# A planned one-core kernel: one fp32 product becomes a transpose with its mean taken on the vector engine, and the planner that writes the order is changed

## The chip, the core and the metric

The kernel runs on one core of a Trainium2 chip. Five engines work side by side and take their own instructions strictly in the order in which they stand: TensorE (PE in the profile; PEld is its weight load), VectorE (DVE), ScalarE (ACT), GpSimd (POOL) and SyncE (SP, which here only issues DMAs). The metric is the device time of one execution in microseconds (us). Before the change it was 2356.49 us, the median of three runs (2355.05 to 2359.45).

## The reference

One decoder layer on 4096 tokens of width 1024, in float32. The input is normalised and projected once; two groups of heads read the projection, their gated outputs are concatenated, projected back, added to the input and normalised.

```python
u = rmsnorm(x, norm_w) @ w_in
# group 1: 4 heads of gated linear attention, chunked
o = gla(q, k, v, decay); gla_out = rms(o) * gla_norm_w * silu(gg)
# group 2: 8 heads of RWKV-7, head size 64
S_t = S_{t-1} (diag(w_t) - kk_t^T (a_t * kk_t)) + v_t^T k_t ;  y_t = S_t r_t
mu = mean(y); var = mean((y - mu)**2)          # over the 64 values of a head
y = (y - mu) * rsqrt(var + eps) * ln_w + ln_b
bonus = sum(r * k * r_k) * v
rwkv_out = (y + bonus) * silu(rg)
out = rmsnorm(x + concat(gla_out, rwkv_out) @ w_out, final_norm_w)
```

Since y is linear in v, the mean over a head's 64 values of y may be taken out of v ahead of the recurrence: with v minus its mean over the 64 values, y comes out with mean zero.

## The kernel before

The 4096 tokens go in 8 blocks of 512 (`TB`). Activations lie transposed, features on partitions. Every projection is three fp16 products (high by high, high by low, low by high), so x and each weight tile are split into a high and a low half; the weights are split once at the start, partly kept in SBUF and otherwise written to DRAM tiles `wdr`, from which they are loaded again for each block into `wr`, `wg` and `wo`. x's two halves of 8 feature tiles lie in four tiles `x16_i_k` of two feature tiles each.

The RWKV heads go in pairs: a unit `u` (0 to 31) is a block and a pair of heads. For a unit, `rwkv_ab` projects k, r, v and the gate, forms scaled keys and queries (`bk`, `DD`), multiplies them (`bank<-DD,bk`), masks the result into `Nb`, and has the triangular 32x32 blocks inverted: `Nb` goes out to DRAM as `nd` and comes back regrouped as `f`, 31 steps of two operations each (`tm`, `Tc`) run on POOL (on DVE for the last unit), and the result goes through `td` back into `Nb`. `rwkv_i` joins the 32x32 blocks to 64x64. `rwkv_c` is the recurrence over the unit's 8 chunks of 64 tokens: per chunk three small fp32 products (`ch<-sv,DD`, `ch<-us,Nb`, `ch<-uv,bk`) with copies on ACT and DVE between them; the states stand in `sv`, and two passes (`y<-DD,sv`, `y<-Nb,uv`) then make y. Unit u+1's chunks need the state that unit u left.

v enters there: `rwkv_ab` takes v (features on partitions), and for each of its four 128-token pieces makes one fp32 product with the constant `c64`, the 64x64 matrix I - 1/64 on the diagonal of a 128x128 tile. That transposes the piece and takes the mean out in one step; four ACT copies then carry the bank into `sv`.

The order of the instructions is not written by hand. The kernel's streams are run once with a model of the engines (`account`, `place`, `Array`); every instruction becomes a `Step` with its duration, its lag and the steps on which it depends. `forward` is a list schedule: it walks through time and lets each engine take the ready step of best rank; `backward` makes ranks from an end time. Before, one forward pass and 13 rounds of backward and forward are made, and the schedule with the earliest modelled end is written out. `parts` says which pieces of a tile the model holds apart: halves of partitions, and for the tiles in `HEADS` also two halves of columns. `keep` (2.0) is how much rank TensorE gives up to stay in the same tile size; `look` (0.15) is how far ahead DVE and ACT look for a better step. All SP entries are DMAs; the model gives each an issue time on SP and a lag until the data can be used. Nearly every instruction is issued by one helper, so the profile shows one line (L408 before, L433 after) and tiles tell them apart.

The last block's output projection (`out_last`) is done in parts: the six feature tiles that are ready first (`bank<-x,wo`, with `halves` scaling them), then the two tiles of the last heads (`bank<-x,x`).

Of the kernel before, what the change touches and what calls it, by code (L numbers as in the profile page):

```python
# [10 lines left out]
F32 = mybir.dt.float32  # L11
# [70 lines left out]
def hymba_kernel(ctx, tc, xT, wt, wg, wo, wua, gup, pk, ck, out):  # L82
# [16 lines left out]
    TABLES = ("pkt", "scl", "invs", "hinv", "mu_s", "omu_s", "carry", "wosc", "woinv", "gnh", "lnh")  # L99
    HEADS = set()  # L100
    now = [0.0]
# [15 lines left out]

# [47 lines left out]
    def account(eng, out, ins, d, lag, cols=0, tiles=None):  # L165
        rdy = lambda k: (lambda r: r[0] - (r[1] == eng) * {"V": 0.075, "S": 0.1, "G": 0.18}.get(eng, 0.0))(ready.get(k, (0.0, "")))
        t = max([0.0] + [rdy(k) for a in ins for k in parts(a)]
                + [used.get(k, 0.0) for k in parts(out)]
                + [rdy(k) for k in parts(out) if eng != "T"])
        if eng == "T":  # L170
            t0, d = array.put(max(t, now[0]), d, cols, tiles)
            t, now[0] = t0, array.free
        else:
            if eng == "D":
                t0 = place("H", t, 0.63)
                t = t0 + 1.28
# [12 lines left out]
    last, turn = [None, 0], [0]  # L189

# [20 lines left out]
    def put(t0, eng, d, lag, cols, tiles, tab, outs, ins, f):  # L211
# [7 lines left out]
        s = Step(len(steps), t0, eng, d, lag, cols, tiles, tab, f)  # L219
        got = lambda m: m.lag + SPARE * (m.eng == "D") - (m.eng == eng) * {"V": 0.075, "S": 0.1, "G": 0.18}.get(eng, 0.0)  # L220
        for k, timed in ki.items():
# [23 lines left out]
    def forward(rank):  # L245

# [3 lines left out]
        left, ready, start = [len(s.on) for s in steps], [0.0] * len(steps), [0.0] * len(steps)  # L250
        end = [0.0] * len(steps)
        for s in steps:
# [7 lines left out]
        for _ in steps:  # L260
# [5 lines left out]
            if e == "T":  # L266
                x = next((x for x in can[e] if run and x[1] == run.n), None)
                x = x or min(heapq.nsmallest(12, can[e]), key=lambda x: x[0] - 2.0 * (steps[x[1]].form == pes.form))
                run = steps[x[1]].next
                can[e].remove(x)  # L270
                heapq.heapify(can[e])
            else:
                x = can[e][0]
                soon = []
                while e in "VS" and wait[e] and wait[e][0][0] <= t + 0.15:
# [12 lines left out]
            if e == "T":  # L288
                start[s.n], d = pes.put(t, d, s.cols, s.tiles)
                end[s.n] = start[s.n] + d  # L290
            elif e == "D":
                free["H"], free["D"] = t + 0.63, max(t + 1.28, free["D"]) + d
                end[s.n] = free["D"]
            else:
# [11 lines left out]
    def backward(end):  # L306
# [7 lines left out]
        for _ in steps:  # L314
# [7 lines left out]
            if e == "T":  # L322
                hold, form = s.d * s.form[0] * s.form[1] / 16 + 0.09 * (s.form != form), s.form
            elif e == "D":
                hold, long = max(0.63, s.d), s.d + 1.28
            free[e], late[s.n] = t + hold, t + long
# [7 lines left out]
    def cost(eng, op, ins, n, o, acc=False):  # L334
# [32 lines left out]
    class Engine:  # L367
# [5 lines left out]
        def __getattr__(self, op):  # L373
            f = getattr(self.eng, op)

            def call(*a, **kw):
# [3 lines left out]
                if aps:  # L380
# [84 lines left out]

    xp = [[sb(big, [P, 2, 2, TB], F16, f"x16_{i}_{k}") for k in range(KT // 2)] for i in range(2)]
    x16 = [[x[k // 2][:, k % 2] for k in range(KT)] for x in xp]
    mfree = {k: [sb(big, [P, TB], F32, f"mg{k}{i}") for i in range(n)] for k, n in NM.items()}
# [14 lines left out]
    bones = sb(one, [P, 32], F32, "bones")  # L483
    c64 = sb(one, [P, P], F32, "c64")
    G.memset(c64, 0.0)
    smask = sb(one, [P, TB], U8, "smask")
# [346 lines left out]
    def rwkv_ab(u, p, b, xs, LR):  # L833
# [511 lines left out]
    def setup():  # L1345
# [28 lines left out]
        for i, t in enumerate(("crs", "rgs")):  # L1374
# [7 lines left out]
            V.tensor_scalar_mul(usc[:, 4 + i:5 + i], usc[:, 2 * i + 1:2 * i + 2], 0.5 / 16384 if i == 0 else 0.5)  # L1382
        for q in (slice(0, 64), slice(64, 128)):
            D.dma_start(c64[q, q], ck[q, CK_C64:CK_C64 + 64])

# [89 lines left out]
    with tc.manual_schedule(engines={getattr(mybir.EngineType, e) for e in ("PE", "DVE", "Activation", "Pool", "SP")}):  # L1475
# [5 lines left out]
        run()  # L1481
        start, end = forward([s.t0 for s in steps])
        start, end = best = forward(backward(end))
# [69 lines left out]
```

## Time and profile before

| | |
|---|---|
| median of 3 runs | 2356.49 us |
| the profiled execution | 2357.35 us |
| its span, first to last instruction | 2355.5 us |
| mean granted TensorE clock | 0.979 of full |
| PE busy | 2245.6 us, 95% |
| DVE busy | 1664.7 us, 71% |
| ACT busy | 1251.0 us, 53% |
| POOL busy | 842.1 us, 36% |
| DMA | 325.46 MB, mean 138 GB/s |
| the chain that ended last | PE 68%, DVE 19%, DMA 5% |

Busy time of PE is time in which at least one product is under way; single products overlap, so the mean duration of one is longer than the time that it adds. The groups list gives for each kind of instruction its count, the busy time that it adds and the mean of one. The windows view gives the same by stretch of the span, with the granted clock.

### The profile page before, as it was taken

How to read it: one execution, taken by the hardware profiler on the slowest of the kernel's cores; microseconds unless marked ns; L12 is line 12 of the kernel's file. 1: busy time of each engine (PE TensorE's matmuls, PEld its weight loads, DVE VectorE, ACT ScalarE, POOL GpSimd, SP SyncE). 2: the span in 40 equal slices, each digit the busy share in tenths (PEclk: the TensorE clock that was granted, in tenths of full speed). 3: DMA queues.
4: the chain of work that ended last, by engine and by line, in shares of the span. 5: the costliest groups of instructions: out<-in, count | busy, mean ns of one | idle time of the engine just before them, and what ended most of it. 6: DMA issues, size and time to landing. Idle time of an engine off the chain costs nothing.

```text
span 2355.5 us, 52166 instructions
## 1 busy us (share of the span) xinstructions
PE 2245.6 (95%) x19432; PEld 1390.7 (59%) x19432; DVE 1664.7 (71%) x3737; ACT 1251.0 (53%) x3229; POOL 842.1 (36%) x2213
## 2 busy tenths in 40 slices
PE   6888999999999999999999999999999989999986
PEld 3556565556665666656575566655666556755643
DVE  7868768478764786757766787638877677676756
ACT  7566765454654655544654546535564455544442
POOL 3450333524334352235425342342514353321400
PEclk9989999999999999999999999999999999999989
DMA  6666545355334543345424553345533454334432
GB/s 195 204 217 213 158 154 157 113 169 152 103 106 125 179 151 93 109 137 174 141 85 121 175 160 97 102 133 173 153 94 106 123 184 137 97 118 127 130 86 76
DMA packets 275523, 325.46 MB, mean 138 GB/s; under 512 B 131732, under 2 KB 132932, under 8 KB 275268
## 3 DMA queue, kind: packets, MB, share of 16 engines
q1 hardware_dynamic: 275268, 322.13, 45.0%
q8 instruction: 152, 2.49, 0.4%
q14 instruction: 103, 0.84, 0.1%
HBM read 276.97 MB, written 45.05 MB: 137 GB/s over the span
## 4 chain that ended last, share of the span: by engine, by line
PE 68%; DVE 19%; DMA 5%; issue 3%; ACT 2%; POOL 2%; SPq 1%; DVEq 0%; ACTq 0%; POOLq 0%
PE bank L408 60%; PE ch L408 6%; PE y L408 2%; DVE DD L408 2%; DVE nta L408 2%; DVE bk L408 1%; POOL tm L408 1%; POOL Tc L408 1%; DVE mgg L408 1%; DVE mgr L408 1%; SPq L408 1%; DMA wdr<-wo 1%; DVE Nb L408 1%; DVE crs L408 1%; DVE sv L408 1%
## 5 line engine op out<-in xcount | busy, mean ns | idle before, releaser
L408 PE MATMUL bank<-x,wr 128*128 128x512 f16 x3264 | 803.1, 380 | 12.5 <-DVE rk L408 4.7
L408 POOL TENSOR_TENSOR tm<-Tc,f 128x60 f32<-128x60 f32 (+24 forms) x961 | 332.4, 346 | 762.3 <-DMA f<-nd 586.0
L408 PEld LDWEIGHTS <-wr 128*128 128x128 f16 x3264 | 317.0, 100 | 308.0 <-issue 21.4
L408 PE MATMUL bank<-x,wg 128*128 128x512 f16 x1536 | 389.6, 383 | 2.4 <-DMA wg<-wdr 2.0
L408 POOL TENSOR_TENSOR Tc<-Tc,tm 128x60 f32<-128x60 f32 (+24 forms) x961 | 341.6, 355 | 73.4
L408 PE MATMUL bank<-x,wo 128*128 128x512 f16 x1488 | 361.9, 384 | 0.6 <-ACT bk L408 0.6
L408 DVE SCALAR_TENSOR_TENSOR sv<-ch,PC,psd 64x64 f32<-64x64 f32 x448 | 126.2, 282 | 195.9 <-PE ch L408 191.0
L408 POOL TENSOR_TENSOR xacc<-xacc,xr 128x512 f32<-128x512 f32 x98 | 131.3, 1340 | 314.8 <-ACT xr L408 215.3
L408 PEld LDWEIGHTS <-wg 128*128 128x128 f16 x1536 | 148.5, 101 | 147.4 <-issue 11.6
L408 PEld LDWEIGHTS <-wo 128*128 128x128 f16 x1488 | 146.0, 101 | 139.9 <-issue 8.0
L408 PEld LDWEIGHTS <-x 128*128 128x128 f16 x3120 | 189.9, 100 | 27.6 <-issue 12.2
L408 PE MATMUL bank<-wg,x 128*128 128x128 f16 x3072 | 199.6, 222 | 4.5 <-DMA wg<-wdr 4.5
L408 ACT ACTIVATE psd<-sv,PC 128x128 f32<-128x128 f32 x256 | 102.2, 399 | 190.1 <-DVE sv L408 152.9
L408 ACT COPY uv<-ch 64x64 f32<-64x64 f32 x512 | 105.5, 206 | 120.5 <-PE ch L408 114.8
L408 ACT COPY us<-ch 64x64 f32<-64x64 f32 x512 | 105.3, 206 | 103.7 <-PE ch L408 93.3
L408 PEld LDWEIGHTS ch<-sv,DD 128*128 128x128 f32 x512 | 91.9, 192 | 49.3 <-DVE sv L408 20.3
L408 PEld LDWEIGHTS ch<-us,Nb 128*128 128x128 f32 x512 | 92.3, 192 | 40.0 <-ACT us L408 10.5
L408 PEld LDWEIGHTS ch<-uv,bk 128*128 128x128 f32 x512 | 92.4, 192 | 39.6 <-ACT uv L408 12.5
L408 PE MATMUL ch<-sv,DD 128*128 128x128 f32 x512 | 105.9, 289 | 8.7 <-DVE sv L408 6.6
L408 ACT ACTIVATE sa<-bank,mu_s 128x512 f32<-128x512 f32 x104 | 71.5, 688 | 73.5 <-PE bank L408 68.5
L408 PE MATMUL ch<-uv,bk 128*128 128x128 f32 x512 | 103.4, 284 | 4.1 <-ACT uv L408 4.0
L408 POOL MEMSET Tc<- 32x8 f32 (+1 forms) x160 | 23.7, 148 | 223.3 <-DMA td<-Tc 182.2
(332 smaller groups left out, 3670.9 us busy)
## 6 DMA issues: line engine op xcount, KB each, us to landing
wr<-wdr SPq DMA_DIRECT2D x256, 256.0 KB
wg<-wdr SPq DMA_DIRECT2D x184, 256.0 KB
xr<-in_xT_dram SPq DMA_DIRECT2D x176, 256.0 KB
wo<-wdr SPq DMA_DIRECT2D x128, 256.0 KB
f<-nd SPq DMA_DIRECT2D x128, 128.0 KB
x<-in_wt_dram SPq DMA_DIRECT2D x29, 512.0 KB
wdr<-wo SPq DMA_DIRECT2D x25, 512.0 KB
out_dram<-mgg SPq DMA_DIRECT2D x33, 256.0 KB
```

What stands on the lines that cost most here:

```text
L408: put(t0, self.name, d, lag, cols, tiles, tab, outs, ins, lambda: f(*a, **kw))
```

## The change

Five things change.

1. In `rwkv_ab` the four products with `c64` become four transposes against the identity. The mean is then taken out on DVE: a reduction of the bank over each 64 values into `vm` (128x8), and one scalar_tensor_tensor that adds -1/64 of it to the bank in place. `c64`, its memset on POOL and its two DMAs go.
2. `put` makes every DMA from an input wait in the model until x's first eight loads have been placed (`lead`).
3. `parts` knows the four parts of an `x16` tile apart (`XS`): two feature tiles by high and low half.
4. The model's figures change: an issue on SP costs 0.5 us (0.63), a DMA 1.15 us more (1.28), the lags depend on what is loaded (reloaded weights 1.1 us instead of 1.6), at most 8 DMAs are under way, POOL's operations cost 0.09 us more, and results that pass between DVE, ACT and TensorE count as ready a little earlier (`early`).
5. After the first pass, five pairs of `keep` and `look` are tried with ten rounds each, and the best of all is taken.

```diff
+        if ap.tensor.name in XS:
+            o = ap.offset % (4 * TB) // TB
+            e = range(o, o + max(1, math.prod(ap.shape[1:]) // TB)) if ap.dtype == F16 else range(4)
+            return [(ap.tensor.name, h, 2 + i) for h in hs for i in e]
...
+    def early(a, b):
+
+        if a not in "VSGT" or b not in "VSGT" or not a:
+            return 0.0
+        if a == b:
+            return {"V": -0.075, "S": -0.1, "G": -0.18, "T": 0.0}[a]
+        return -0.045 if a == "T" else -0.09 if b == "T" else -0.07
...
+        if eng == "D" and ins[0].tensor.name.startswith("in_"):
+            if ins[0].tensor.name.startswith("in_xT") and len(lead) < KT:
+                lead.append(s)
+            else:
+                for m in lead:
+                    s.follow(m, None)
...
-                free["H"], free["D"] = t + 0.63, max(t + 1.28, free["D"]) + d
+                if len(flight) > 7:
+                    start[s.n] = t = max(t, flight[-8])
+                free["H"], free["D"] = t + 0.5, max(t + 1.15, free["D"]) + d
...
-            return 0.14 + 0.07 * few + n * (2.13 if len(big) > 1 else 0.95) / 960 + 0.34 * (n == 8)
+            return 0.23 + 0.07 * few + n * (2.13 if len(big) > 1 else 0.95) / 960 + 0.34 * (n == 8)
...
-                        d, lag = max(0.01, b / 3.6e5), 1.6 if ins[0].space == DRAM else 0.6
+                        d = max(0.01, b / 3.6e5)
+                        if ins[0].space == DRAM:
+                            lag = {"wdr": 1.1, "in": 1.9 if b > 4e5 else 1.1, "td": 1.2}.get(ins[0].tensor.name.split("_")[0].rstrip("0123456789"), 1.7)
+                        else:
+                            lag = 2.1 if b > 2e5 else 1.2 if o.shape[-1] == 32 else 0.6
...
         for c in range(4):
-            T.matmul(pv[:, c], lhsT=v[:, P * c:P * c + P], rhs=c64, start=True, stop=True)
-
+            T.transpose(pv[:, c].rearrange("p h t -> p (h t)"), v[:, P * c:P * c + P], ident)
+        vm = sb(rt, [P, 8, 1], F32, "vm", 1)
+        pu = pv.rearrange("p c h t -> p (c h) t")
+        V.tensor_reduce(vm, pu, op=ALU.add, axis=AX.X)
+        V.scalar_tensor_tensor(pu, vm.broadcast_to((P, 8, 64)), -1.0 / 64, pu, ALU.mult, ALU.add)
...
-        for _ in range(12):
-            start, end = forward(backward(end))
-            best = min(best, (start, end), key=lambda x: max(x[1]))
+        first_order = forward([s.t0 for s in steps])
+        best = first_order
+        for keep, look in ((0.5, 0.15), (0.5, 0.3), (0.7, 0.3), (1.0, 0.15), (2.0, 0.3)):
+            start, end = first_order
+            for _ in range(10):
+                start, end = forward(backward(end), keep, look)
+                best = min(best, (start, end), key=lambda x: max(x[1]))
```

The whole order is new, on every engine. Three places of it follow.

SP at the program's start, before. `mgg` and `mgr` hold x's eight feature tiles of block 0, `x_1_..` two raw weight tiles.

```order
L408 DMA mgg_0_88<-in_xT_dram 128x512
L408 DMA x_1_0_0_80<-in_wt_dram 128x1024
L408 DMA mgr_0_89<-in_xT_dram 128x512
L408 DMA x_1_1_0_81<-in_wt_dram 128x1024
L408 DMA mgr_0_90<-in_xT_dram 128x512
L408 DMA mgr_0_91<-in_xT_dram 128x512
L408 DMA f_0_216<-in_wg_dram 128x8x16
```

The same place after the change.

```order
L433 DMA mgg_0_88<-in_xT_dram 128x512
L433 DMA mgr_0_89<-in_xT_dram 128x512
L433 DMA mgr_0_90<-in_xT_dram 128x512
L433 DMA mgr_0_91<-in_xT_dram 128x512
L433 DMA x_1_0_0_80<-in_wt_dram 128x1024
L433 DMA x_1_1_0_81<-in_wt_dram 128x1024
L433 DMA f_0_215<-in_wg_dram 128x8x16
```

The two weight tiles of 512 KB have moved behind x's last three tiles of 256 KB.

DVE some 20 us into the program, before: `nva`, `nyg` and `nta` are x's inverse norm by Newton steps, `amW`, `pw` and `scl` a weight tile's scale, `wr<-x_1` the low half of a split weight.

```order
L408 TENSOR_SCALAR nva_207<-bank_0_183 128x128
L408 TENSOR_SCALAR nyg_208<-nva_207 128x128
L408 TENSOR_TENSOR nta_209<-nyg_208 128x128
L408 TENSOR_REDUCE amW_210<-bank_0_183 128x1
L408 TENSOR_SCALAR pw_206<-amW_210 128x1
L408 TENSOR_SCALAR pw_206<-pw_206 128x1
L408 SCALAR_TENSOR_TENSOR wr_215<-x_1_1_0_81,scl_179,wr_214 128x1024
L408 TENSOR_SCALAR scl_179<-pw_206 128x1
L408 SCALAR_TENSOR_TENSOR nta_209<-nta_209,nva_207 128x128
```

The same after the change.

```order
L433 TENSOR_SCALAR nva_206<-bank_0_182 128x128
L433 TENSOR_SCALAR nyg_207<-nva_206 128x128
L433 TENSOR_TENSOR nta_208<-nyg_207 128x128
L433 SCALAR_TENSOR_TENSOR nta_208<-nta_208,nva_206 128x128
L433 SCALAR_TENSOR_TENSOR nyg_207<-nta_208,nyg_207 128x128
L433 TENSOR_TENSOR nta_208<-nyg_207 128x128
```

The Newton steps have moved ahead of the weights' scales and splits; both `wr` splits now stand between the Newton steps and the first use of x's norm.

PE near the program's end, before: the first chunks of unit 30 (`ch`), with v's last product (`c_0,v`), the gates' projections (`wg`) and the output projection (`wo`).

```order
L408 MATMUL ch_266<-us_267,Nb_0_135 128x64
L408 LDWEIGHTS wg_233
L408 MATMUL bank_0_186<-x_1_3_0_83,wg_233 128x512
L408 MATMUL bank_0_183<-c_0_99,v_201 128x128 x3
L408 MATMUL ch_266<-uv_134,bk_242 128x128
L408 MATMUL bank_0_183<-c_0_99,v_201 128x128
L408 MATMUL ch_266<-sv_255,DD_0_132 128x128
L408 MATMUL ch_266<-us_267,Nb_0_135 128x64
L408 MATMUL ch_266<-uv_134,bk_242 128x128
L408 MATMUL ch_266<-sv_255,DD_0_132 128x128
```

The same chunks after the change, from the end of the first one.

```order
L433 MATMUL ch_266<-uv_133,bk_241 128x128
L433 LDWEIGHTS wr_212
L433 MATMUL bank_0_182<-x_1_3_0_83,wr_212 128x512
L433 MATMUL ch_266<-sv_254,DD_0_131 128x128
L433 MATMUL bank_0_183<-ident_102,amo_281 128x128
L433 MATMUL ch_266<-us_267,Nb_0_134 128x64
L433 MATMUL ch_266<-uv_133,bk_241 128x128
L433 LDWEIGHTS wo_138
L433 MATMUL bank_0_187<-x_0_0_0_76,wo_138 128x512
L433 LDWEIGHTS wo_139
L433 MATMUL bank_0_186<-x_0_0_0_76,wo_139 128x512
L433 MATMUL ch_266<-sv_254,DD_0_131 128x128
```

Before, chunks two to four of unit 30 stand without other products between them and the first `wo` product comes in the fifth; after, the first `wo` products stand in the second chunk and go on between the chunks from there.

More of the change, by code (lines that the diff above doesn't have):

```diff
@@ L99, in hymba_kernel @@
     TABLES = ("pkt", "scl", "invs", "hinv", "mu_s", "omu_s", "carry", "wosc", "woinv", "gnh", "lnh")
-    HEADS = set()
+    HEADS, XS = set(), set()
     now = [0.0]
@@ L174, in account @@
             if eng == "D":
-                t0 = place("H", t, 0.63)
-                t = t0 + 1.28
+                t0 = place("H", t, 0.5)
+                t = t0 + 1.15
             t = place(eng, t, d)
@@ L185, in account @@
         return t0
+    def early(a, b):
[4 more added lines that the diff above has]
+        return -0.045 if a == "T" else -0.09 if b == "T" else -0.07
     table = [0]
     steps, wkey, rkey, wlast, readers = [], {}, {}, {}, {}
-    last, turn = [None, 0], [0]
+    last, turn, lead = [None, 0], [0], []
     def whole(ap):
@@ L250, in forward @@
         left, ready, start = [len(s.on) for s in steps], [0.0] * len(steps), [0.0] * len(steps)
-        end = [0.0] * len(steps)
+        end, flight = [0.0] * len(steps), []
         for s in steps:
@@ L267, in forward @@
                 x = next((x for x in can[e] if run and x[1] == run.n), None)
-                x = x or min(heapq.nsmallest(12, can[e]), key=lambda x: x[0] - 2.0 * (steps[x[1]].form == pes.form))
+                x = x or min(heapq.nsmallest(12, can[e]), key=lambda x: x[0] - keep * (steps[x[1]].form == pes.form))
                 run = steps[x[1]].next
@@ L274, in forward @@
                 soon = []
-                while e in "VS" and wait[e] and wait[e][0][0] <= t + 0.15:
+                while e in "VS" and wait[e] and wait[e][0][0] <= t + look:
                     r, n = heapq.heappop(wait[e])
@@ L291, in forward @@
             elif e == "D":
-                free["H"], free["D"] = t + 0.63, max(t + 1.28, free["D"]) + d
+                if len(flight) > 7:
+                    start[s.n] = t = max(t, flight[-8])
+                free["H"], free["D"] = t + 0.5, max(t + 1.15, free["D"]) + d
                 end[s.n] = free["D"]
+                flight.append(end[s.n] + s.lag)
             else:
@@ L324, in backward @@
             elif e == "D":
-                hold, long = max(0.63, s.d), s.d + 1.28
+                hold, long = max(0.5, s.d), s.d + 1.15
             free[e], late[s.n] = t + hold, t + long
@@ L466, in hymba_kernel @@
     xp = [[sb(big, [P, 2, 2, TB], F16, f"x16_{i}_{k}") for k in range(KT // 2)] for i in range(2)]
+    XS.update(t.tensor.name for x in xp for t in x)
     x16 = [[x[k // 2][:, k % 2] for k in range(KT)] for x in xp]
@@ L483, in hymba_kernel @@
     bones = sb(one, [P, 32], F32, "bones")
-    c64 = sb(one, [P, P], F32, "c64")
-    G.memset(c64, 0.0)
     smask = sb(one, [P, TB], U8, "smask")
@@ L1481, in hymba_kernel @@
         run()
-        start, end = forward([s.t0 for s in steps])
-        start, end = best = forward(backward(end))
-        for _ in range(12):
-            start, end = forward(backward(end))
-            best = min(best, (start, end), key=lambda x: max(x[1]))
+        first_order = forward([s.t0 for s in steps])
[5 more added lines that the diff above has]
+                best = min(best, (start, end), key=lambda x: max(x[1]))
         start, end = best
```

8 lines of the change are left out of this document (3 added, 5 removed).

## The prediction

> **What bounds the kernel now.** I read the page first, then the busy time by stretch, then the groups, the waits and the timeline at both ends.
>
> ```profile
> span 2355.5 us, 52166 instructions
> PE 2245.6 (95%) x19432; PEld 1390.7 (59%) x19432; DVE 1664.7 (71%) x3737; ACT 1251.0 (53%) x3229; POOL 842.1 (36%) x2213
> ...
> core 0: us, PE busy (x) PEld busy (x) DVE busy (x) ACT busy (x) POOL busy (x), PEclk, DMA share, GB/s
> 0.00:24.00 24.00, 10.86 (x83) 5.98 (x84) 12.38 (x45) 11.69 (x18) 10.28 (x32) 1.00 0.93 294
> 24.00:80.00 56.00, 48.47 (x235) 23.05 (x234) 51.63 (x133) 40.19 (x73) 16.28 (x13) 0.91 0.46 141
> 80.00:300.00 220.00, 196.36 (x1776) 129.15 (x1775) 177.03 (x470) 145.91 (x321) 78.69 (x201) 0.93 0.63 197
> 300.00:2200.00 1900.00, 1862.91 (x16243) 1154.79 (x16241) 1325.70 (x2840) 999.77 (x2670) 715.48 (x1912) 0.99 0.44 134
> 2200.00:2250.00 50.00, 47.65 (x504) 31.65 (x503) 37.30 (x100) 15.93 (x35) 21.37 (x55) 0.99 0.28 79
> 2250.00:2300.00 50.00, 41.83 (x301) 25.53 (x300) 25.62 (x76) 22.29 (x73) 0.00 (x0) 0.81 0.37 100
> 2300.00:2355.00 55.00, 37.51 (x303) 20.59 (x301) 35.03 (x78) 15.26 (x41) 0.00 (x0) 0.90 0.21 72
> ```
>
> The columns are the stretch, its length, and each engine's busy time with its instructions. From 300 to 2200 us TensorE is busy 98% of the time (1862.9 of 1900): there the kernel is TensorE's work, and work taken from it shortens the span unless a new wait replaces it. TensorE's idle time lies mostly at the ends: 13 us before 24 us, 31 from 24 to 300, 25 after 2250, where the granted clock also falls to 0.81. From 24 to 80 us DVE is busy 92% of the time. So there are three limits: DVE at the start, TensorE in the middle, and a chain of dependent steps at the end.
>
> **v's products become transposes.** The old product is the group `c,v`; `ident,bk` is a transpose of the same size that the kernel already makes.
>
> ```profile
> L408 PE MATMUL bank<-c,v 128*128 128x128 f32 x256 | 37.0, 278 | 0.0
> L408 PE MATMUL bank<-ident,bk 128*128 128x128 f32 x256 | 37.8, 277 | 2.2 <-DVE DD L408 2.2
> ...
> 2252.20 0.83 PE L408 MATMUL bank<-c,v 128*128 128x128 f32 x6
> ...
> 2229.21 0.82 PE L408 MATMUL bank<-ident,bk 128*128 128x128 f32 x6
> ```
>
> A unit makes 4 products, so 32 units make 128, and they have 256 rows: an fp32 product runs as two. A unit makes 8 transposes of `bk`, 256 in all, with 256 rows: one each. By busy time a product costs 37.0/128 = 0.289 us and a transpose 37.8/256 = 0.148. The change saves 128 x 0.141 = 18.1 us by this count. The timeline gives the other bound: six rows in a run take 0.83 and 0.82 us, of which the last one's own 0.28 is tail, so a row adds 0.11 us in either group, a product two rows, a transpose one: 128 x 0.11 = 14.1 us. I take 16, the middle, since the four stand in short runs. It all lies in TensorE's full stretch or in the first 300 us. The constant's memset and two DMAs go as well, from POOL and SP, where TensorE waits for neither. The Trainium skill, "TensorE: Matmul & The Clock Gate", section Terms, says that transpose mode is four times faster for FP32; by it a transpose would cost 0.072 us and the saving be 27.8. The trace says half, not a quarter, and the trace has the kernel's own transposes.
>
> **The mean on DVE.** New per unit: a reduction of 128x512 from PSUM, and one scalar_tensor_tensor that reads and writes PSUM.
>
> ```profile
> L408 DVE TENSOR_REDUCE amW<-crs 128x1 f32<-128x512 f32 x1 | 0.7, 676 | 0.0
> L408 DVE SCALAR_TENSOR_TENSOR rgs<-rgs,bank 128x512 f32<-128x512 f32 x32 | 21.9, 683 | 28.1 <-ACT rgs L408 27.8
> L408 DVE SCALAR_TENSOR_TENSOR r<-r,pkt,kf 128x512 f32<-128x512 f32 x32 | 26.2, 818 | 0.1
> ...
> PE bank L408 <- DVE bk L408: 14.7, 10, 4.3
> ...
> PE ch L408 <- DVE sv L408: 6.6, 11, 1.8
> ```
>
> No row of the trace writes PSUM from DVE. The nearest are 0.683 (reading PSUM) and 0.818 (the slowest of this shape), so the pair costs 1.36 to 1.50; I take 1.40, near the row that reads PSUM. That is 45 us over 32 units, and DVE goes from 1664.7 to about 1710 us, 73%. Its result, `sv`, is needed only when the unit's chunks begin, and those wait for the unit's inverse, 62 operations on POOL later; so the pair itself hides, and so does the bank that it holds 1.4 us longer, one of six (if it is wanted sooner, the 1.4 us fall on TensorE, within the bounds below). What it costs is queueing: behind it on DVE stand `bk` and `sv`, for which TensorE already waits 14.7 and 6.6 us. DVE's free time shrinks by 45 of 691 us, 7%, which alone would add 1.5 us to those two waits; at worst one pair in four falls ahead of something that TensorE is waiting for (8 x 1.4 = 11 us). I take +3 in the middle stretch, bounds 0 and 11.
>
> **The start.** Three of x's loads stood behind weights; the order now has all eight first.
>
> ```profile
> 0.75 2.28 SPq L408 DMA_DIRECT2D mgg<-in_xT_dram  x5
> ...
> 3.55 0.63 ACT L408 ACTIVATE rk<-mgg 128x512 f32<-128x512 f32 x1 [1.32 <-DMA mgg<-in_xT_dram]
> ...
> 7.31 0.63 ACT L408 ACTIVATE kf<-mgg 128x512 f32<-128x512 f32 x1 [0.27 <-DMA mgg<-in_xT_dram]
> ...
> 13.69 0.61 ACT L408 ACTIVATE uv<-mgr 128x512 f32<-128x512 f32 x1
> ...
> 15.41 0.28 DVE L408 TENSOR_SCALAR nva<-bank 128x128 f32<-128x128 f32 x1
> ...
> 17.18 1.28 DVE L408 SCALAR_TENSOR_TENSOR wr<-x,scl,wr 128x1024 f16<-128x1024 f32 x1
> ...
> 22.41 2.07 DVE L408 SCALAR_TENSOR_TENSOR mgg<-mgg,nwx,bank 128x512 f32<-128x512 f32 x3 [0.81 <-PE bank L408]
> ```
>
> x's fifth square starts at 7.31 when its load lands; the eighth waits until 13.69. With three more loads of about 0.94 us each (the first five squares start between 3.55 and 7.31) it could start at 10.1, 3.6 us sooner, and the Newton steps with it. But the two weight splits of 1.28 us and the scales now stand between Newton and x's first scaling at 22.41, and their weights land later. I count about 6.8 us of DVE work there, from about 14.0, so x's first scaling comes near 21: a gain of 1.5, bounds 3.6 and -1. Against it DVE, full from 24 to 80 us and 80% busy to 300, gets the pair for four units, 5.6 us, of which I put 2 on the path (bounds 0 and 5.6). Together +0.5.
>
> **The order.** Counted along the PE order, the tile size changes 657 times instead of 633.
>
> ```profile
> 2239.75 0.59 PE L408 MATMUL bank<-x,wg 128*128 128x512 f16 x2
> 2239.98 0.21 DVE L408 TENSOR_TENSOR tm<-Tc,f 128x52 f32<-128x52 f32 x1
> ...
> 2240.27 0.24 PE L408 MATMUL bank<-Ta,Nb 32*32 32x32 f32 x2
> ...
> 2241.70 3.19 PE L408 MATMUL bank<-x,wg 128*128 128x512 f16 x14
> ```
>
> In the run of 14 an fp16 product adds 0.216 us ((3.19 - 0.38)/13); two of them ahead of a 32x32 product take 0.52 from start to start, so a change costs about 0.09: +2 us for 24 more. Of the 37 us that TensorE idles from 300 to 2200, most at block boundaries, x's parts held apart and the new lags may save some: I take -3, bounds 0 and -9.
>
> **The end.** Unit 30's chunks set it, and the inverse that they wait for.
>
> ```profile
> 2195.93 0.24 POOL L408 TENSOR_TENSOR tm<-Tc,f 128x31 f32<-128x31 f32 x1 [45.56 <-DMA f<-nd]
> ...
> 2224.32 0.22 POOL L408 TENSOR_TENSOR Tc<-Tc,tm 128x8 f32<-128x8 f32 x1
> ...
> 2246.21 0.43 DVE L408 STREAM_TRANSPOSE Ta<-Nb 32x256 f32<-32x256 f32 x1
> ...
> 2251.66 0.48 PE L408 MATMUL ch<-us,Nb 128*128 128x64 f32 x2
> ...
> 2271.42 0.90 DVE L408 STREAM_TRANSPOSE Ta<-Nb 32x256 f32<-32x256 f32 x2
> 2272.27 4.75 PE L408 MATMUL bank<-x,wo 128*128 128x512 f16 x13
> ```
>
> Unit 30's inverse leaves POOL at 2224.5, but its transpose runs at 2246.2, among unit 31's inverse steps on DVE, and its chunks go on at 2251.66, bare, while TensorE idles and its clock falls: 13 `wo` products then take 4.75 us instead of 3.0. In the new order both transposes stand ahead of unit 31's inverse on DVE and `wo` products fill from the second chunk. But unit 31's inverse then starts later, and its own transposes (2271.42 now, about 10 us ahead of their use) become next to late. Of the 8 us idle and 2 us of slow clock from 2250 to 2300 I take half, -5; bounds -12 (some of the 17 idle us after 2300 too) and +3.
>
> **The sum.** -16 +3 +0.5 +2 -3 -5 = -18.5. The profiled execution took 2357.35 us, its span 2355.5 and 1.85 around it; it lies 0.9 above the median of the runs. 2357.35 - 18.5 gives 2339.
>
> **Rivals.**
> A. The new order pays in full: start -3.6, middle -9, end -12, v -18.1, against +2 +3 +2. That is -36, 2321; the case reaches from there to 2331, with 2326 as its middle. For it: idle time at both ends is 69 us. Against: a new order also makes new waits.
> B. DVE takes most of it back: +11 in the middle and +5.6 at the start, and the end gains nothing: -16 +11 +4 +2 -3 = -2, 2355. For it: DVE is full at the start. Against: from 300 to 2200 us it is idle 30% of the time.
> C. The transposes run as two rows like the products, so nothing is saved: -2.5, also 2355. Against it stands `ident,bk` with one row each.
> D. Slower: weights arrive late. The planner now takes reloaded weights as usable 0.5 us sooner, so SP issues them later, and TensorE waits where it now hardly does.
>
> ```profile
> PE bank L408 <- DMA wg<-wdr: 6.5, 4, 2.9
> ...
> wr<-wdr SPq DMA_DIRECT2D x256, 256.0 KB
> wg<-wdr SPq DMA_DIRECT2D x184, 256.0 KB
> ```
>
> Four waits of 1.6 us occur now. With 12 more the gain is gone, beyond 15 it is slower; at 20, one load in 22, +32: 2371. Against it: x's first five loads were issued in 2.28 us, 0.46 each, as the new figure of 0.5 for an issue has it.
> E. Slower: the clock. If each unit's transposes let the clock fall once, as after 2251, each time costs some 1.8 us (4.75 against 3.0): 32 x 1.8 = 57, 2396. Against it: from 300 to 2200, with eight `bk` transposes in every unit, the clock is 0.99. The Trainium skill, same page, section "Part 4: PE-mode transpose", says that a transpose does not count as PE-busy for the clock gate in the same way. That is this rival; the trace does not bear it out.
>
> **How the numbers follow.** The forecast (2332 to 2348 as its own range) gets 0.53, A 0.18, B 0.12, C 0.05, D 0.10, E 0.02. About 0.2% (4.7 us) is what a measurement here can tell from no change. B's upper half counts as the same with C, B's lower half as faster: faster 0.53 + 0.18 + 0.06 = 0.77, same 0.06 + 0.05 = 0.11, slower 0.12. The range goes down to 2322, past A's middle, and up to 2354, into B; D, E and a little of A, B and C stay out, some 0.2.
>
> **What would show it.** Right: a group `ident,v` with 128 rows and about 19 us busy instead of 37.0; two new DVE groups of 32 near 0.7 us each; DVE near 1710 us; TensorE's idle time from 300 to 2200 near 37 us or below; the clock from 2250 to 2300 us above 0.81. Wrong: `ident,v` with 256 rows (C); waits of PE for DMA `wg` or `wr` beyond 25 us (D); waits for `bk` and `sv` beyond 32 us (B); a granted clock below 0.97 in the middle (E).

## The result and the profile after

| | before | after |
|---|---|---|
| median | 2359.0 us (12 runs, 2355.1 to 2366.8) | 2356.2 us (12 runs, 2346.3 to 2361.7) |
| ratio to before | 1 | 0.9986, 95% interval 0.9974 to 0.9999 |
| the profiled execution, its span | 2357.35, 2355.5 us | 2360.01, 2358.2 us |
| mean granted clock there | 0.979 | 0.981 |

By the ratio the change brings 3.3 us, 0.14% (interval 0.2 to 6.1 us). The forecast was 18.5 us. The profiled execution of after lies 3.8 us above the median of its runs, so its span is longer than that of before although the kernel is a little faster; small differences between the two traces are read with that in mind.

The page of the changed kernel and its windows, the same stretches as before:

```profile
span 2358.2 us, 52000 instructions
PE 2237.5 (95%) x19304; PEld 1358.8 (58%) x19304; DVE 1712.8 (73%) x3801; ACT 1252.5 (53%) x3229; POOL 861.3 (37%) x2212
...
0.00:24.00 24.00, 10.52 (x83) 5.42 (x84) 12.95 (x47) 12.98 (x20) 10.27 (x32) 1.00 0.90 277
24.00:80.00 56.00, 42.87 (x207) 19.89 (x208) 49.74 (x127) 38.52 (x70) 15.60 (x13) 0.91 0.40 128
80.00:300.00 220.00, 202.19 (x1758) 130.24 (x1758) 180.09 (x473) 147.99 (x320) 79.75 (x202) 0.94 0.66 202
300.00:2200.00 1900.00, 1852.88 (x16041) 1121.32 (x16038) 1362.02 (x2882) 991.63 (x2645) 732.35 (x1901) 0.99 0.44 133
2200.00:2250.00 50.00, 49.88 (x577) 35.44 (x577) 39.10 (x83) 22.70 (x60) 23.29 (x67) 1.00 0.41 125
2250.00:2300.00 50.00, 40.18 (x337) 24.24 (x334) 30.99 (x108) 21.44 (x68) 0.00 (x0) 0.90 0.35 101
2300.00:2358.20 58.20, 38.94 (x320) 22.30 (x317) 37.90 (x88) 17.20 (x50) 0.00 (x0) 0.85 0.20 68
```

TensorE's busy time fell by 8.1 us, not by 16, and its idle time over the span grew from 109.9 to 120.7 us. It grew where I had expected it to shrink: from 300 to 2200 us it is 47.1 us (1900 - 1852.88) and was 37.1. After 2250 us it is 29.1 us (9.8 up to 2300 and 19.3 behind) and was 26.2.

The groups of the changed kernel for what is new:

```profile
L433 PE MATMUL bank<-ident,v 128*128 128x128 f32 x128 | 21.3, 274 | 0.0
L433 DVE TENSOR_REDUCE vm<-bank 128x8 f32<-128x512 f32 x32 | 22.0, 688 | 17.6 <-PE bank L433 15.8 <-ACT uv L433 1.5
L433 DVE SCALAR_TENSOR_TENSOR bank<-vm,bank 128x512 f32<-128x512 f32 x32 | 22.2, 692 | 0.7
```

The transposes are 128 rows with 21.3 us where the products were 256 with 37.0: 15.7 us less. A transpose costs 0.166 us and a product 0.289, a factor of 1.74. The Trainium skill, "TensorE: Matmul & The Clock Gate", section Terms, gives a factor of four for FP32. This trace does not show it either. The pair on DVE is 1.38 us, 44.2 us in all. Both are near the forecast (about 19 us of transposes, and 1.40 us a pair).

The waits of TensorE in the changed kernel (what it waited for, us in total, times, longest):

```profile
PE ch L433 <- DVE sv L433: 19.0, 17, 8.2
PE bank L433 <- DVE bk L433: 6.8, 3, 6.3
PE bank L433 <- DMA wg<-wdr: 6.4, 9, 1.7
PE bank L433 <- DMA wr<-wdr: 0.3, 1, 0.3
```

Waits for `sv` and `bk` are 25.8 us together and were 21.3; weights are no later than before.

The timeline of the changed kernel at both ends (start, length, engine):

```profile
9.55 0.63 ACT L433 ACTIVATE uv<-mgr 128x512 f32<-128x512 f32 x1
...
21.41 0.74 DVE L433 SCALAR_TENSOR_TENSOR mgg<-mgg,nwx,bank 128x512 f32<-128x512 f32 x1
...
2245.95 0.89 DVE L433 STREAM_TRANSPOSE Ta<-Nb 32x256 f32<-32x256 f32 x2
...
2252.45 0.33 PE L433 MATMUL ch<-us,Nb 128*128 128x64 f32 x2
...
2252.69 0.19 DVE L433 TENSOR_TENSOR tm<-Tc,f 128x31 f32<-128x31 f32 x1 [2.28 <-DMA f<-nd]
...
2273.53 2.75 PE L433 MATMUL bank<-x,wo 128*128 128x512 f16 x12
...
2286.10 0.90 DVE L433 STREAM_TRANSPOSE Ta<-Nb 32x256 f32<-32x256 f32 x2
```

The same step of unit 31's inverse in the kernel before, its first on DVE:

```profile
2237.63 0.19 DVE L408 TENSOR_TENSOR tm<-Tc,f 128x31 f32<-128x31 f32 x1 [2.88 <-DMA bcdb<-brow]
```

x's eighth square starts at 9.55 (it was 13.69; 10.1 was expected) and x's first scaling at 21.41 (22.41; 21). At the end unit 30's two transposes now stand together ahead of unit 31's inverse, which begins at 2252.69 (2237.63 before), but they run no sooner than the second of them did before (2246.21). Unit 31's own transposes come at 2286.10 and were at 2271.42. 12 `wo` products take 2.75 us at a granted clock of 1.00 (2273.5 to 2276.4 us); before, 13 took 4.75 at 0.63 (2272.2 to 2277.1).

### The profile page after: what moved, and what is told of

It is laid out like the page before. It is cut to its first block, busy times and chain, and to the rows that moved or that the text cites. A ratio compares the mean times of both kernels' runs of the same rounds, so it can differ in the third digit from the quotient of the medians.

```text
span 2358.2 us, 52000 instructions
## 1 busy us (share of the span) xinstructions
PE 2237.5 (95%) x19304; PEld 1358.8 (58%) x19304; DVE 1712.8 (73%) x3801; ACT 1252.5 (53%) x3229; POOL 861.3 (37%) x2212
## 4 chain that ended last, share of the span: by engine, by line
PE 61%; DVE 25%; DMA 7%; ACT 4%; issue 2%; SPq 1%; POOL 0%; DVEq 0%; ACTq 0%; POOLq 0%
PE bank L433 53%; PE ch L433 6%; DVE DD L433 3%; PE y L433 2%; DVE nta L433 2%; DVE bk L433 2%; DVE x L433 1%; DVE Nb L433 1%; SPq L433 1%; DMA wg<-wdr 1%; DMA xr<-in_xT_dram 1%; DVE mgr L433 1%; DVE mgg L433 1%; DVE sv L433 1%; DVE crs L433 1%
## 5 line engine op out<-in xcount | busy, mean ns | idle before, releaser
L433 POOL TENSOR_TENSOR tm<-Tc,f 128x60 f32<-128x60 f32 (+24 forms) x961 | 350.9, 365 | 621.5 <-DMA f<-nd 487.7
L433 PE MATMUL bank<-x,wg 128*128 128x512 f16 x1536 | 382.0, 383 | 3.2 <-DMA wg<-wdr 2.1
L433 PEld LDWEIGHTS ch<-us,Nb 128*128 128x128 f32 x512 | 87.3, 193 | 45.1 <-ACT us L433 27.7
```

The source lines that it names most:

```text
L433: put(t0, self.name, d, lag, cols, tiles, tab, outs, ins, lambda: f(*a, **kw))
```

## Experiments

All runs are compared with the kernel before, run beside them on the same chip; us are the ratio less one, times 2359. A ratio is known to about 0.0015, so two of them differ by more than chance from about 5 us on. Where the order of the instructions is kept on every engine, only the named instructions differ.

**The edit to v in a fixed order.** Four kernels fill a table: old and new order, products or transposes, with and without the pair. In the first two the old planner plans the products, and the instruction is exchanged when it is issued; in the other two the new planner plans transposes and pair. Without the pair the mean of v is left out of the computation: in e2 and e3, which have transposes, and in e4, whose products are with the identity.

```
# e1, e2: the old kernel and its order
  T.matmul(pv[:, c], lhsT=v[...], rhs=c64, start=True, stop=True)
+ steps[-1].f = lambda: nc.tensor.transpose(pv[:, c], v[...], ident)
# e1 only: the first S.copy(sv...) of a unit issues the pair on DVE ahead of itself
# e3, e4: the changed kernel and its order
  V.tensor_reduce(vm, ...)            ; + steps[-1].f = lambda: None
  V.scalar_tensor_tensor(pu, vm, ...) ; + steps[-1].f = lambda: None
# e4 only
  T.transpose(pv[:, c], v[...], ident)
+ steps[-1].f = lambda: nc.tensor.matmul(pv[:, c], lhsT=v[...], rhs=ident, ...)
```

> The sequence of the kernel before on every engine, but each of v's products is issued as a transpose in the same place, and the reduction and the subtraction of the mean stand on DVE ahead of the unit's first copy to sv. Theory P (the saving on v is there, and the new order loses it again): about -16 from the transposes and +0 to +3 from the pair, so 2340 to 2343 where the kernel before has 2356. Theory Q (DVE's 44 us of pairs take the saving back by delaying sv and bk): within 4 us of the kernel before. Theory R (a shorter row of TensorE is not time saved, since other waits fill it): within 4 us, and the next run too.

> The same, but the mean of v is left out of the computation: transposes in the old places and nothing more on DVE. P: -16, 2340, equal to the run before this within 3 us. Q: -16, 2340, some 12 us below the run before this. R: within 4 us of the kernel before.

> The changed kernel with its own sequence on every engine, but the two DVE instructions of each mean are not issued (the mean of v is left out of the computation). P: 0 to 3 us below the changed kernel, so 2351 to 2355. Q: about 12 us below it, 2342. R: like the changed kernel.

> The changed kernel's own sequence on every engine, the mean left out as before, and each of v's transposes issued as an fp32 product with the identity in the same place. With the run before this it prices the products in the new order. P: +14 to +18 over the run before this, so about 2368, 12 us slower than the kernel before with the same products: that is the new order's own cost. Q: the new order is as good as the old or better, so 2351 to 2357. R: like the run before this.

| | old order | new order |
|---|---|---|
| products, no pair | 0 (the kernel before) | 1.0057 (1.0041 to 1.0073): +13.4 us |
| transposes, no pair | 0.9997 (0.9985 to 1.0008): -0.7 | 0.9984 (0.9972 to 0.9997): -3.8 |
| transposes and pair | 1.0139 (1.0123 to 1.0156): +32.8 | 0.9986 (the changed kernel): -3.3 |

In the new order everything goes as theory P has it: the transposes bring 17.2 us, the pair costs 0.5, and the order itself, with the old work in it, is 13.4 us slower than the old one. In the old order nothing does: the transposes bring 0.7 us and the pair, unplanned, costs 33.5. Theory R has e2 right (within 4 us of the kernel before) and misses e1 and e4.

The table can be read along another way: with transposes and no pair the new order is not slower than the old one but 3.1 us faster (-3.8 against -0.7). So neither the order nor the transposes have a price of their own here. What the table gives without choosing a way is the two together: -3.8 us.

The timeline has this unit by unit. The last unit's gate scaling on DVE (`rgs<-rgs,bank`) in the kernel before, then e2, e1, e4, e3 and after:

```profile
2227.29 0.69 DVE L408 SCALAR_TENSOR_TENSOR rgs<-rgs,bank 128x512 f32<-128x512 f32 x1 [3.90 <-ACT rgs L408]
```

```profile
2220.99 0.69 DVE L408 SCALAR_TENSOR_TENSOR rgs<-rgs,bank 128x512 f32<-128x512 f32 x1 [3.82 <-ACT rgs L408]
```

```profile
2260.11 0.69 DVE L408 SCALAR_TENSOR_TENSOR rgs<-rgs,bank 128x512 f32<-128x512 f32 x1 [3.91 <-ACT rgs L408]
```

```profile
2258.08 0.68 DVE L433 SCALAR_TENSOR_TENSOR rgs<-rgs,bank 128x512 f32<-128x512 f32 x1
```

```profile
2241.18 0.68 DVE L433 SCALAR_TENSOR_TENSOR rgs<-rgs,bank 128x512 f32<-128x512 f32 x1
```

```profile
2249.73 0.68 DVE L433 SCALAR_TENSOR_TENSOR rgs<-rgs,bank 128x512 f32<-128x512 f32 x1
```

From e4 to e3 the same instruction comes 16.9 us sooner; from before to e2 only 6.3, and 39.1 later from e2 to e1. (Between the old and the new order the step stands at another place among the other work, so those rows are not to be compared.) In the profiled executions TensorE's busy time falls by 12.0 us from before to e2 (2245.6 to 2233.6), and its idle time grows by 5.0; the profiled execution of e2, 2350.36 us, is the fastest of its 12 runs, whose median is 2358.8. From e4 to e3 busy time falls by 20.4 (2250.3 to 2229.9) and idle time grows by 2.4.

So idle time is the smaller part of what sets the two orders apart. The granted clock goes with the rest: over all runs its mean is 0.9794 before and 0.9772 in e2, but 0.9803 in e4 and 0.9825 in e3. If TensorE's 2240 us of busy time stretch as the clock falls (an estimate from these figures; the last section has runs where it does not come out), 0.0022 is 5 us each way, together 10 of the 16.5 us between 17.2 and 0.7. Why the clock goes down with the same exchange in one order and up in the other was not tried.

Why the pair is so dear in the old order is seen in the waits, of ScalarE first and then of TensorE, in e1:

```profile
ACT sv L408 <- DVE bank L973: 58.2, 30, 7.0
...
PE ch L408 <- ACT us L408: 13.1, 16, 1.9
```

and in those of e2 and of the changed kernel:

```profile
PE ch L408 <- ACT us L408: 4.7, 9, 1.0
```

```profile
ACT sv L433 <- DVE bank L433: 12.8, 10, 3.8
```

`bank` from L973 is the pair's result. In e1 ScalarE stands at the copies to `sv` in 30 of 32 units, 1.9 us each time, until the pair is done; whatever is queued behind them on ScalarE waits too, the chunks' copies `us` among it, and TensorE's wait for `us` grows from 4.7 to 13.1 us. Where the pair was planned the copies wait 12.8 us in all. So a planned pair hides and an unplanned one holds up ScalarE's queue; theory Q, which had DVE's load itself as the price, falls with e3, where leaving the pair out brings 0.5 us and not 12. How the 33.5 us divide is not shown: TensorE's wait for `sv`, which DVE writes, grows too, from 10.2 us in e2 to 16.8, and no run separates ScalarE's queue from DVE's own steps behind the pair.

**The parts alone, each with its own planner.** e5 is the kernel before with v's edit only (the five new lines in `rwkv_ab`, `c64` gone); e6 is the changed kernel with v's old product and `c64`.

> The kernel before with v by transposes and its mean on DVE, and nothing else changed: the old planner plans the two new DVE steps and draws its own order (13 list schedules, old figures, no lead for x, x's parts not apart). What is known: in the new order the transposes save 17 and the mean costs 1 to 3, and that order with the old products takes 13 more than the kernel before; in the old order, unplanned, the mean costs 32. Theory S (the new planner's rules make a worse order): this one keeps the old rules, so about -15, 2344. Theory T (any newly drawn order loses some 10 us against the one that was kept before, whatever the rules): about -3, 2356, like the changed kernel. Theory U (DVE's mean costs more where the planner's old figures place it): slower than before.

> The changed kernel with v by the old products and their constant, planned as such: the new planner alone (x's lead, x's parts apart, new figures, best of 51 list schedules). S: about +13, 2372. T: also slower, +5 to +15. If the new order's 13 us come only from being planned around short transposes, it is within 4 us of the kernel before.

e5: 1.0056 (1.0040 to 1.0071), +13.2 us. e6: 1.0107 (1.0089 to 1.0126), +25.2 us. Each half alone is slower, the two together a little faster: the parts don't add up. Theory S, by which the old rules keep the saving, falls with e5, and e6 lies 12 us above what S gives for it. T misses as well: by T e5 should have come near 2356, and it came at 2371, and e6 at +5 to +15. U fits e5's time, but in e5's trace ScalarE's copies to `sv` wait 11.2 us for the pair, no more than in the changed kernel (12.8), which speaks against it. What is common to e4, e5 and e6 is an order that differs from the kernel before's.

**Other orders of the same work.** If near-equal orders differ by 10 us on the chip, one measured order says little of an edit. Eight orders of the changed kernel, same instructions, same rules; they differ in which of the planner's list schedules is written out.

```
# e7: one setting only; e10, e15 to e18 likewise, with another setting or one of its other rounds
- for keep, look in ((0.5, 0.15), (0.5, 0.3), (0.7, 0.3), (1.0, 0.15), (2.0, 0.3)):
+ for keep, look in ((0.7, 0.3),):
# e8: the old search
- the loop over five settings
+ start, end = best = forward(backward(end)), then 12 more rounds at keep=2.0, look=0.15
# e9: the kernel before; the round that held the best is passed over
+ best = (start, end) if i == 5 else min(best, (start, end), key=...)
```

> The changed kernel, but the best is taken from the ten list schedules of one of its five settings (0.7, 0.3), which the planner's model puts 0.2 us behind the one that the changed kernel takes: the same work and the same rules, another order. S: within 4 us of the changed kernel, 2352 to 2360. T: it may lie 5 to 15 us to either side.

> The changed kernel with the old search (13 list schedules, the form bonus 2.0 and the look-ahead 0.15), all other rules new. If the wider search has picked an order that flatters the model: 5 to 10 us below the changed kernel, about 2348. S (the new figures and dependences are at fault): within 4 us of the changed kernel. T: to either side.

> The kernel before, with the order that its own planner puts second (0.1 us behind by its model) in place of the first: the same work, the same rules. Theory T (which of the near-equal orders is drawn decides some 10 us, and the order kept before was a good draw): slower than the kernel before, by 5 to 15, 2364 to 2374; its TensorE work stays as it was (2246 within 4) and the idle time grows from 110 us. Against T: within 4 us of the kernel before.

> The changed kernel with a third order, from the same setting as the one that it takes (1.0, 0.15), 0.3 us behind by the planner's model. T: another draw, between 2340 and 2365, with TensorE's busy time near 2235 as in the other orders, and the difference in its idle time. Against T: within 4 us of the changed kernel.

> The changed kernel with the best of the ten schedules of the setting (0.5, 0.3); the planner's model puts it 2.7 us behind. Theory L (a look-ahead of 0.3 on DVE and ScalarE makes the better orders): 2335 to 2350. Theory T (a draw): anywhere from 2340 to 2375.

> The changed kernel with the best of the ten schedules of the setting (0.5, 0.15); the planner's model puts it 6.5 us behind. L: 2355 to 2375, like the three orders with the short look-ahead so far (2356, 2363, 2373). T: anywhere from 2340 to 2375.

> The changed kernel with the second-best of the schedules of the fast order's own setting (0.7, 0.3). Theory L (the longer look-ahead makes the better orders): between 2335 and 2357, as the two so far. Theory T (a draw): as likely above 2357 as below.

> The changed kernel with the second-best of the schedules of the setting (0.5, 0.3). L: between 2335 and 2357. T: as likely above 2357 as below; with both above, L falls.

Busy, idle (span less busy) and clock are those of the profiled execution.

| order (`keep`, `look`) | ratio to before (95%) | us | TensorE busy | idle | clock |
|---|---|---|---|---|---|
| e7 (0.7, 0.3) | 0.9934 (0.9919 to 0.9949) | -15.6 | 2231.6 | 108.9 | 0.985 |
| the changed kernel (1.0, 0.15) | 0.9986 (0.9974 to 0.9999) | -3.3 | 2237.5 | 120.7 | 0.981 |
| e15 (0.5, 0.3) | 0.9994 (0.9978 to 1.0010) | -1.4 | 2234.7 | 119.7 | 0.982 |
| e18 (0.5, 0.3) | 1.0001 (0.9985 to 1.0017) | +0.2 | 2237.9 | 124.4 | 0.980 |
| e8 (2.0, 0.15) | 1.0015 (1.0004 to 1.0027) | +3.5 | 2235.9 | 125.9 | 0.982 |
| e17 (0.7, 0.3) | 1.0019 (1.0003 to 1.0034) | +4.5 | 2235.9 | 125.6 | 0.981 |
| e10 (1.0, 0.15) | 1.0053 (1.0038 to 1.0069) | +12.5 | 2244.0 | 125.1 | 0.979 |
| e16 (0.5, 0.15) | 1.0082 (1.0065 to 1.0099) | +19.3 | 2242.2 | 130.7 | 0.981 |

The eight lie 35 us apart, with a mean of +2.5. Three that the planner's model holds within 0.3 us of each other (the changed kernel, e7, e10) came out at -3.3, -15.6 and +12.5. The kernel before's own second order, e9, is 1.0031 (1.0019 to 1.0043), 7.3 us slower than its first, within what T expected (5 to 15); its busy time moved by 2 us (2247.9) and its idle time from 109.9 to 119.0. So the draw of the order matters with both planners, and by more than T had said: e10 (median 2372.7) lies above T's 2340 to 2365 and its busy time moved too (2244.0, not near 2235), and e16 (2375.6) lies at the upper end of T's range. The wider search as the fault falls with e8, which is slower than the changed kernel and not 5 to 10 us faster. Theory L falls by its own mark, since e17 and e18 (medians 2364.2 and 2358.7) both lie above 2357; e15 (2357.2) had already missed L's 2335 to 2350. The four orders with the longer look-ahead have a mean of -3.1 and the four with the shorter +8.0, but the groups overlap; whether the setting helps a little stays open with four draws each.

The windows of the fastest order, e7, and of e10, at the same stretches:

```profile
80.00:300.00 220.00, 203.88 (x1837) 131.93 (x1834) 185.04 (x481) 149.48 (x325) 80.97 (x203) 0.96 0.67 207
300.00:2200.00 1900.00, 1861.39 (x16197) 1134.62 (x16195) 1371.48 (x2903) 1000.45 (x2671) 746.05 (x1946) 1.00 0.45 134
2250.00:2300.00 50.00, 47.89 (x359) 28.19 (x357) 26.14 (x64) 23.19 (x79) 0.00 (x0) 0.96 0.35 106
```

```profile
80.00:300.00 220.00, 202.93 (x1704) 128.09 (x1702) 178.02 (x468) 145.81 (x319) 77.85 (x202) 0.93 0.66 202
300.00:2200.00 1900.00, 1847.64 (x16064) 1123.95 (x16059) 1364.22 (x2880) 987.12 (x2630) 729.00 (x1900) 0.99 0.45 132
2250.00:2300.00 50.00, 39.67 (x247) 22.09 (x246) 34.47 (x112) 20.23 (x61) 0.74 (x5) 0.86 0.37 97
```

From 300 to 2200 us TensorE idles 38.6 us in e7, 47.1 in the changed kernel and 52.4 in e10, and from 2250 to 2300 it idles 2.1, 9.8 and 10.3. It is not one stall: in the middle, pauses of up to 1.2 us make 20.5 us in e7, 27.2 in the changed kernel and 26.2 in e10, and the longer ones 18.1, 19.9 and 26.2, of which the longest are 2.1, 3.6 and 4.9. Against the changed kernel, e7 lost mostly short pauses.

**Does v's edit cost the same in the fast order?** e13 and e14 are e3's and e4's edits made to e7.

> The order of the second-best run (2342) on every engine, the two DVE instructions of each mean not issued (the mean of v is left out of the computation). In the changed kernel's order this gave 0 to 3 us, in the old order 32. If the mean hides wherever it was planned in: 2337 to 2342. If the price of a DVE step depends on the order: anything down to 2320.

> The same order, the mean left out, and each of v's transposes issued as an fp32 product with the identity in the same place. If TensorE's row count is what the transposes save wherever TensorE is the limit: 14 to 18 over the run before this one, about 2355, as in the changed kernel's order. If the old order's result (1 us) is the rule and 17 the exception: within 5 us of the run before this.

e13: 0.9942 (0.9925 to 0.9960), -13.7 us; e14: 0.9982 (0.9972 to 0.9993), -4.2 us. So the pair costs nothing here either (-1.9 to e7, inside the error), and the transposes bring 9.4 us (busy time 2244.5 to 2231.4, idle time 106.3 to 106.6). With the two other orders that is 17, 9 and 1 us for one and the same exchange, each known to about 5 us: 17 and 1 differ clearly, 9 only little beyond the error from either.

**One of the new rules undone.** In the orders made by the new rules TensorE's weight loads wait for the chunks' copies `us` far more often; before, the changed kernel and e11, from 300 to 2200 us:

```profile
PEld ch L408 <- ACT us L408: 4.4, 10, 1.0
```

```profile
PEld ch L433 <- ACT us L433: 20.2, 75, 1.5
```

```profile
PEld ch L433 <- ACT us L433: 8.1, 19, 1.0
```

```
# e11; e12 also keeps only the setting (1.0, 0.15)
  def early(a, b): ...
-     return -0.045 if a == "T" else -0.09 if b == "T" else -0.07
+     return 0.0
```

> The changed kernel with one rule undone: the planner again takes a result from another engine as usable at its lag, not 0.045 to 0.09 us sooner. In the four orders made with the new rule TensorE's weight loads of the chunks wait for us 72 to 94 times between 300 and 2200 us, in the orders of the old rule 10 to 21 times. Theory H (the new rule sets the chunk steps too close, and this is what the new order loses): those waits fall to 10 to 25, and the time to 2340 to 2348. T: the waits fall, but the time is one more draw, 2340 to 2365.

> The same rule undone, and the best of only the ten schedules of the setting that the changed kernel's order came from (1.0, 0.15): a second draw without the new rule. H: 2340 to 2348 as well. T: another draw, which may lie on the other side of the changed kernel than the run before this one.

The waits fell, from 75 to 19 times and to 21 in e12, and the time rose: 1.0078 (1.0065 to 1.0091), +18.4 us, and 1.0102 (1.0086 to 1.0118), +24.1. Theory H falls: these waits are not what the new order loses. T's range, up to 2365, is missed too (2378 and 2386). TensorE's idle time from 300 to 2200 us grew to 62.8 and 67.6 us, from 47.1. Both draws without the rule are slower than seven of the eight with it; that suggests that the rule helps, and two draws don't show it.

## Why the prediction was wrong, by its steps

- **v's transposes, -16.** Rows and busy time came as forecast (-15.7). That all of it would be time, because it "lies in TensorE's full stretch", does not hold in every order: 17.2, 9.4 and 0.7 us. What in the order decides it was not settled. In the profiled executions only 2.4, 0.3 and 5.0 us of it came back as idle time, and the estimate from the granted clock covers 10 of the 16.5 us between the first and the last; neither was taken apart by a run.
- **The mean on DVE, +3 (0 to 11).** Planned, it measured +0.5 and -1.9, which within the error is nothing. The reason that I gave was incomplete: the cover is not only that `sv` is wanted late, but that the planner places the pair ahead of ScalarE's copies. Where it stands bare it costs 33.5 us, three times my upper bound, in part at least through ScalarE's queue, which I had not named.
- **The start, +0.5.** x's squares and first scaling moved as forecast (9.55 and 21.41). TensorE was busy 5.6 us less from 24 to 80 us (48.47 to 42.87) and 5.8 more from 80 to 300, so up to 300 us its busy time is the same.
- **The order: tile sizes +2, middle -3, end -5, and their sum with the -16.** This is the step that failed. With the start I had the new order at -5.5 and added it to v's -16 as if the two were independent. Transposes and new order together should have given -21.5; they measure -3.8 (e3). These 17.7 us, less 2.5 by which the pair cost less than +3, are the whole miss of 15.2. How the 17.7 divide depends on the way through the table: with the old products the new order costs 13.4 instead of saving 5.5, and the transposes then bring 17.2; put into the old order, the transposes bring 0.7 instead of 16, and the new order then saves 3.1. I took the places at which the order looked better (x's parts, unit 30's transposes) and added up what each could save, as if the rest stayed; but the whole order is drawn anew, and the sum had no term for the draw, which spreads over 35 us.
- **Middle and end by the trace.** From 300 to 2200 us TensorE's idle time went up by 10 us instead of down by 3; e4, the new order with products, has 44.9 us there, so most of the rise is there without the transposes. At the end unit 30's transposes run at 2245.95, as late as the second of them did before, though they do stand ahead of unit 31's inverse; that inverse begins 15 us later than before, and its transposes come 14.7 us later, the risk that I had put at 3 us. After 2250 us TensorE idles 2.9 us more instead of less. That the clock from 2250 to 2300 us would rise above 0.81 came true (0.90). The tile sizes don't explain why the new orders differ: the fast order e7 and the changed kernel have 657 changes each, and e8, slower than both, has 625. Whether the 24 changes more than before cost the 2 us was not measured. What in the order makes the idle time stays open.
- **The rivals.** A, the order paid in full, and B, DVE taking it back, both fell (B's mark was waits beyond 32 us; they are 25.8, and the pair costs 0.5). C fell with the 128 rows, D with 6.7 us of waits for weights, E with a clock of 0.99 in the middle. B and C gave the time that came, 2355, but neither mechanism is what happened; that is luck. The rival that was missing is that the new order may be worse for the same work. The only mark that warned of it was TensorE's idle time "near 37 us or below"; it is 47.1.

The best version found is e7: 2342.4 us, 0.9934 of before and 12 us below the changed kernel, the same work in the planner's second-best order. It is one order picked out of eight on the chip, not a rule that would find the next one.

## What to carry to other kernels

Where a planner writes out the order, an edit has two effects, its own work and a new draw of the order; price the work by exchanging instructions in a fixed order, in more than one order since the price itself changed (17, 9 and 1 us), and give the draw a spread taken from several orders of the same kernel (here 35 us) before adding up what single places seem to gain. When the best few schedules lie closer together than the planner's model is wrong, run them on the chip instead of taking the first. And a busy share of 98% doesn't promise that saved work is saved time: count it in full only with a measurement in the order at hand.

## What the runs showed of the hardware

The same 19304 TensorE rows have a busy time of 2231.6 us at a mean granted clock of 0.985 (e7) and of 2244.0 at 0.979 (e10): 12.4 us, where 0.006 of 2240 is 13. So these two orders differ not in idle time alone. It is not a rule: e5, with as many rows, has 2233.3 us at 0.978, and e6, with 19432 rows at 0.985, has 2246.3 us where the kernel before has 2245.6 at 0.979. In a single run of products it is plain: 12 `wo` products took 2.75 us at a clock of 1.00 and 13 took 4.75 at 0.63. From 2250 to 2300 us the clock is 0.96 with 2.1 us idle in e7 and 0.86 with 10.3 in e10, but 0.81 with 8.2 in the kernel before and 0.90 with 9.8 in the changed one. Whether the pauses lower the clock or both come from something else was not tried. A DVE pair of 1.38 us, placed directly ahead of a copy at which ScalarE already stands, cost about 1 us of the whole program's time for each of its 32 uses (33.5/32); placed earlier by the planner, in two other orders, it cost nothing that could be measured.
